# A trunk of two attention layers: a fixed TensorE order for the first attention, gates spread over its groups, and four shared PSUM banks

## Chip, cores and metric

The kernel runs on one core of a Trainium2 chip. The metric is the device time in microseconds (us), of which the median over runs is given. The engines are TensorE (PE in the profile, its weight loads PEld), VectorE (DVE), ScalarE (ACT), GpSimd (POOL) and SyncE (SP, which issues the transfers). All times of the trace come from one profiled execution.

## What is computed

A residual stream x of 512 positions by 1024 channels goes through two layers in f32. Cut to what matters:

```
# layer 1: multi-head latent attention (16 heads of 64 + 32 rotary channels)
proj = rmsnorm(x) @ w_in                      # c_q 384, c_kv 256, k_rope 32, gate 1024
q = rmsnorm(c_q) @ w_q_up                     # 16 heads x 96
k_nope, v = split(rmsnorm(c_kv) @ w_kv_up)    # 16 heads x 64 each
k = concat(k_nope, k_rope of all heads)
q, k = rmsnorm per head, then rope on the last 32
o = causal_softmax_attention(q, k, v)         # 4 blocks of 128 queries
x = x + (o * silu(gate)) @ w_out
x = x + sigmoid(x @ ple_w_gate) * (p @ ple_w_proj)      # embedding part
k_sh, v_sh = split(rmsnorm(x) @ w_kv_shared)
# layer 2: stick-breaking attention on k_sh, v_sh
q, gate = split(rmsnorm(x) @ w_in)
x = x + (stick_breaking(q, k_sh, v_sh) * silu(gate)) @ w_out
x = x + sigmoid(x @ ple_w_gate) * (p @ ple_w_proj)
```

## The kernel before

**Products.** Activations lie transposed: channels on the 128 partitions, 512 positions along the free axis. Every f32 product is three TensorE products of rounded halves, hi x hi, hi x lo and lo x hi (`mm3`, L136). The halves of a weight tile come from `split_w` (L142): ScalarE rounds (`wh`, L147), then VectorE or GpSimd, whichever `lo_engine` names, subtracts (`wl`, L148). A gemm chunk (`gemm_gen`, L179) loads one weight tile `ws`, splits it, multiplies it with eight activation tiles into one PSUM bank and evacuates it. `yield` cuts it into steps that a caller can place between other work.

**Stages.** `mla_in` (L313, to about 41 us) computes c_q and c_kv and ends with the sums of squares (`stats`, L374) and the row R of 1/rms (`row_of`, L202, used by the gate evacuations). `k_rope` (L404) computes the shared rotary part of k. `mla_group(g)` (L453) computes q, k and v of four heads: four query chunks of nine products and four kv chunks of six. Between and behind them lies a chain on other engines: sums of squares on VectorE, a power on GpSimd (`rq`, L478, and `rk`, L505), rope on GpSimd (L308 to L311), and multiplications of k on VectorE (L511, L513). Only then can the heads be transposed. Group 0 and four of the eight gate chunks (`GATES[0]` = 4) are computed ahead of the attention.

**First attention** (`layer`, L787, about 77 to 270 us). It runs over 64 pairs of head and query block in turns. In a turn stand, each for a later pair than the one behind it: for the first block of a head the transposes of its q and k (`mla_prep`, `head_t`, L523, tag t), the scores and the softmax (`mla_front`, L581, tag s), the transposes of the normalised weights `e` (`pt_evac`, L538, tag t, evacuated by L553 and L554), and at the last block the value products of the head (`av`, L556, tag o, evacuated by L574 and L575). Between them, steps of other work are drawn from a generator: the next group, gates, and halves of the output projection. This places instructions only in the program; a scheduler decides the order on each engine from priorities. Attention work has one (`MLA_PRIO`, 50 ahead), and fill products have one behind (`MLA_FILL`).

**PSUM.** There are eight banks: two each of g and s, three of t, and one of o. The bank o holds one value product at a time, in both attentions, and `row_of` and the statistics too.

**The rest.** Output projection and embedding (`out_ple`, `pp_gemm`, 270 to 345 us), then the second attention (`sb_layer`, L682, 388 to 617 us), then the output again. In the second attention TensorE's order is not left to the scheduler: with `lin` set, `pe` (L120) ties each product or transpose to the one before. Its turns name quotas of fill steps at six places.

Of the kernel before, what the change touches and what calls it, by code (L numbers as in the profile page):

```python
# [56 lines left out]
SPREAD_PLE = "gstt"  # L57
# [26 lines left out]
class Trunk:  # L84
    def __init__(self, ctx, tc, A):
# [9 lines left out]
    BUFS = {"A": 8, "B": 10, "qk": 8, "hat": 6, "gate": 8, "v": 2, "f": 6, "e": 12, "ws": 3, "wh": 2, "wl": 2, "R": 1,  # L95
            "sm": 16, "smg": 3, "g": 2, "s": 2, "t": 3, "o": 1}
# [82 lines left out]
    def gemm_gen(self, w_dram, m, acts, evac, gain=None, k0=0, k1=NK, parts=1, fine=False):  # L179
# [10 lines left out]
        for i in range(parts):  # L190
            cs = slice(i * w, (i + 1) * w)
            ps = self.gps([P, w])
            for k in range(nk):
                xh, xl = acts[k0 + k]
                with self.pri(self.mp):
                    self.mm3(ps, wh[:, k], wl[:, k], xh[:, cs], xl[:, cs], k == 0, k == nk - 1)
                if (fine or k == NK // 2 - 1) and k < nk - 1:
                    yield
# [3 lines left out]
    def row_of(self, col):  # L202
        nc = self.nc
        ps = self.ps([P, S], "o")
# [108 lines left out]
    def mla_in(self):  # L313
# [60 lines left out]
        sps = self.ps([P, 3, NT], "o")  # L374
# [78 lines left out]
    def mla_group(self, g, res):  # L453
# [7 lines left out]
        for t in range(NT):  # L461
            ts = slice(t * P, (t + 1) * P)
            ps = self.gps([P, GH * QK])
            for k in range(3):
                ch, cl = self.cq[k]
                with self.pri(self.mp):
                    self.mm3(ps, ch[:, ts], cl[:, ts], wqh[:, k], wql[:, k], k == 0, k == 2)
# [20 lines left out]
        for t in range(NT):  # L488
            ts = slice(t * P, (t + 1) * P)
            ps = self.gps([P, 2, GH, HD])  # L490
            for k in range(2):
                ch, cl = self.ckv[k]
                with self.pri(self.mp):
                    self.mm3(ps, ch[:, ts], cl[:, ts], wkh[:, k], wkl[:, k], k == 0, k == 1)
# [28 lines left out]
    def head_t(self, src, hh, scale):  # L523
        nc = self.nc
        ps = self.ps([QK, S], "t")
        for t in range(NT):
            nc.tensor.transpose(ps[:, t * P:(t + 1) * P], src[hh // 2][:, t, hh % 2], self.ident)  # L527
# [28 lines left out]
    def av(self, h, V):  # L556
# [3 lines left out]
        ps = self.ps([P, S], "o")  # L560
# [43 lines left out]
    def sb_group(self, g, res):  # L604
# [13 lines left out]
        for m in (2 * g, 2 * g + 1):  # L618
            yield from self.gemm_gen(A["w_k"][m], m, self.x2, k_evac, gkv, fine=True)
            yield  # L620
        for m in (2 * g, 2 * g + 1):
            yield from self.gemm_gen(A["w_sq"][m], m, self.x2, q_evac, gsb, fine=True)
# [103 lines left out]
    def pp_gemm(self, i, halves=(0, 1), early="B", fine=False):  # L726
# [7 lines left out]
        for half in halves:  # L734
# [3 lines left out]
            for mc in range(4):  # L738
                ps = self.gps([P, S])
                for k in range(2):  # L740
                    xh, xl = pacts[k]
                    self.mm3(ps, wh[:, mc, k], wl[:, mc, k], xh, xl, k == 0, k == 1)
                    if fine and k == 0:
                        yield
# [3 lines left out]
                if fine or mc % 2:  # L748
                    yield

    def out_half(self, m, w_out, resid, tag):
# [7 lines left out]
        self.gemm_chunk(w_out[m], m, self.og, evac, k0=0, k1=NK // 2)  # L759
# [27 lines left out]
    def layer(self, windows, prep, front, pair, prep_lead, lead, av_lag, off):  # L787
        hp = self.tc.high_priority
# [3 lines left out]
        done = [0] * NG  # L792
        for i in range(-prep_lead, NS + lead + av_lag):
            ip = i + prep_lead
            if ip < NS:
                g = ip // GS
                if ip % NT == 0:
                    with hp(offset=off[0]):
                        heads[ip // NT] = prep(ip // NT, *self.groups[g])
                n, gen = windows[g]  # L800
                while done[g] * GS < n * (ip % GS + 1):
                    next(gen, None)
                    done[g] += 1
                if ip % GS == GS - 1:
                    for _ in gen:
                        pass
            if 0 <= i < NS:
                with hp(offset=off[1]):
                    es[i] = front(i // NT, i % NT, *heads[i // NT])
            b = i - lead  # L810
            if 0 <= b < NS:
                h, j = divmod(b, NT)
                if j > 0:
                    with hp(offset=off[2]):
                        self.pt_evac(h, j - 1, es.pop(b), es.pop(b - 1) if j == 1 else None)
            c = b - av_lag
            if 0 <= c < NS and c % NT == NT - 1:
                h = c // NT
                with hp(offset=off[3]):
                    self.av(h, heads[h][-1])  # L820
                if h % 2:
                    pair(h // 2)

    def chain(self, *parts):
        for p in parts:
            if callable(p):
                p()
                yield
            else:
# [191 lines left out]
```

## Time and profile before

| | |
|---|---|
| median of 3 runs | 712.2 us (709.18 to 715.35) |
| the profiled execution | 711.81 us |
| its span | 710.0 us, 10006 instructions |
| mean granted TensorE clock | 0.975 |
| TensorE busy | 674.5 us, 95% |
| first attention, 77.1 to 270.0 | 192.9 us |
| second attention, 385 to 600 | 215.0 us of it |

A busy TensorE is not one at its best: products overlap, so a row's duration is longer than the distance to the next. The clock is the share of full speed that the throttle granted. In a row, `g<-A,wh` reads output tile from input tiles, and `[1.77 <-DVE gate L575]` says that the engine had been idle for 1.77 us until VectorE's instruction of line 575 ended.

### The profile page before, as it was taken

What the parts mean: (1) busy time and instruction counts of PE and PEld (TensorE: products, weight loads), DVE (VectorE), ACT (ScalarE), POOL (GpSimd) and SP (SyncE); (2) the same over time, 40 slices, a digit from 0 to 9 for tenths busy, and PEclk for the clock granted to TensorE, in tenths of its full rate; (3) what the DMA queues carried; (4) which work ended last, traced back from release to release, by engine and by line L of the source; (5) the groups of instructions that cost most, each with busy time, mean ns of one, the idle gap of its engine ahead of it and who ended that gap; (6) DMA issues with size and microseconds to landing.
All of it is one profiled execution on the core that took longest, in us unless ns stands there. A gap on an engine that the chain in (4) does not pass through costs nothing.

```text
span 710.0 us, 10006 instructions
## 1 busy us (share of the span) xinstructions
PE 674.5 (95%) x3558; PEld 563.7 (79%) x3558; DVE 485.6 (68%) x931; ACT 402.0 (57%) x807; POOL 358.0 (50%) x293
## 2 busy tenths in 40 slices
PE   9799999999979999999899999999999998899997
PEld 6588888879868888888688788778788676688886
DVE  6748499979976865646655777876886797744432
ACT  7256596958986855354434567556565566422321
POOL 5729566755795441036642755663673776100131
PEclk9999999989998999999899999999999999899999
DMA  6242212000023222545232222122111223143231
GB/s 232 57 142 92 89 35 63 30 31 16 16 72 109 88 60 75 163 131 164 95 93 86 87 60 61 59 80 70 60 59 44 77 90 118 60 132 105 88 120 60
DMA packets 21617, 59.81 MB, mean 84 GB/s; under 512 B 2880, under 2 KB 3392, under 8 KB 21568
## 3 DMA queue, kind: packets, MB, share of 16 engines
q1 hardware_dynamic: 21568, 59.18, 26.5%
q8 instruction: 28, 0.46, 0.3%
q14 instruction: 21, 0.17, 0.1%
HBM read 54.97 MB, written 4.19 MB: 83 GB/s over the span
## 4 chain that ended last, share of the span: by engine, by line
PE 61%; DVE 17%; issue 11%; ACT 6%; POOL 2%; DMA 2%; SPq 0%; ACTq 0%; DVEq 0%; POOLq 0%
PE g L131 32%; PE s L131 11%; PE t L131 9%; PE o L131 4%; DVE e L678 3%; PE t L134 3%; DVE wl L148 3%; ACT wh L147 1%; DVE ptl L554 1%; PE t L527 1%; DVE e L590 1%; ACT e L594 1%; DMA e<-in_xT 1%; DVE A L168 1%; DVE A L165 1%
## 5 line engine op out<-in xcount | busy, mean ns | idle before, releaser
L131 PE MATMUL g<-A,wh 128*128 128x512 f32 x576 | 189.7, 411 | 11.0 <-DVE gate L437 4.9
L147 ACT CAST wh<-ws 128x1024 fp32r<-128x1024 f32 (+2 forms) x92 | 90.5, 983 | 112.7 <-issue 53.3
L131 PEld LDWEIGHTS g<-A,wh 128*128 128x128 f32 x576 | 105.4, 194 | 35.6 <-issue 8.3
L148 DVE TENSOR_TENSOR wl<-ws,wh 128x1024 fp32r<-128x1024 f32 (+2 forms) x72 | 99.8, 1387 | 48.6 <-ACT wh L147 46.9
L131 PE MATMUL g<-A,wl 128*128 128x512 f32 x288 | 115.0, 404 | 2.3 <-DVE wl L148 1.9
L186 POOL TENSOR_TENSOR ws<-ws,gc 128x1024 f32<-128x1024 f32 x24 | 51.7, 2156 | 60.1 <-DMA ws<-in_w_sq 29.2
L679 POOL TENSOR_TENSOR e<-e,e 128x384 f32<-128x384 f32 (+1 forms) x48 | 61.7, 1303 | 22.0 <-DVE e L678 14.3
L553 ACT CAST pth<-t 128x384 fp32r<-128x384 f32 (+1 forms) x96 | 49.3, 518 | 40.6 <-PE t L134 40.0
L131 PEld LDWEIGHTS g<-A,wl 128*128 128x128 f32 x288 | 55.6, 194 | 15.3 <-DVE wl L148 2.4
L554 DVE TENSOR_TENSOR ptl<-t,pth 128x384 fp32r<-128x384 f32 (+1 forms) x96 | 56.4, 592 | 14.1 <-ACT pth L553 13.9
L134 PE MATMUL t<-ident,e 128*128 128x128 f32 x320 | 55.5, 274 | 1.3 <-DVE sm L596 1.1
L678 DVE TENSOR_TENSOR_SCAN e<-e,maskb 128x384 f32<-128x384 f32 (+1 forms) x32 | 49.7, 1593 | 8.3 <-ACT e L667 8.2
L148 POOL TENSOR_TENSOR wl<-ws,wh 128x1024 fp32r<-128x1024 f32 (+2 forms) x20 | 41.8, 2088 | 25.8 <-ACT wh L147 25.7
L131 PE MATMUL t<-A,wh 128*128 128x512 f32 x160 | 50.3, 395 | 0.0
L131 PE MATMUL o<-pth,v 128*128 128x256 f32 (+2 forms) x128 | 43.5, 350 | 5.0 <-DVE gate L575 4.9
L134 PEld LDWEIGHTS t<-ident,e 128*128 128x128 f32 x320 | 40.6, 141 | 9.0 <-issue 1.5
L594 ACT ACTIVATE e<-e,sm,smg 128x128 f32<-128x128 f32 (+1 forms) x64 | 42.1, 660 | 8.5 <-DVE sm L593 8.2
L131 PE MATMUL g<-wh,B 128*128 128x384 f32 (+1 forms) x136 | 44.1, 379 | 2.6 <-DVE v L521 2.6
L131 PE MATMUL s<-qk,qk 96*128 96x256 f32 (+2 forms) x192 | 43.2, 340 | 0.8 <-ACT qk L531 0.8
L598 POOL TENSOR_SCALAR e<-e,sm 128x384 f32<-128x384 f32 (+3 forms) x48 | 29.8, 627 | 25.7 <-DVE sm L596 24.2
L131 PE MATMUL g<-wh,A 128*128 128x256 f32 x208 | 42.8, 289 | 0.0
L781 POOL TENSOR_TENSOR f<-f,hat 128x512 f32<-128x512 f32 x4 | 7.3, 1828 | 70.0 <-ACT f L779 70.0
(295 smaller groups left out, 1617.0 us busy)
## 6 DMA issues: line engine op xcount, KB each, us to landing
ws<-in_w_pg SPq DMA_DIRECT2D x16, 512.0 KB, 3.5
ws<-in_w_g SPq DMA_DIRECT2D x8, 512.0 KB, 3.2
ws<-in_w_o SPq DMA_DIRECT2D x16, 256.0 KB, 2.6
ws<-in_w_k SPq DMA_DIRECT2D x8, 512.0 KB, 3.5
ws<-in_w_sq SPq DMA_DIRECT2D x8, 512.0 KB, 3.6
ws<-in_w_v SPq DMA_DIRECT2D x8, 512.0 KB, 3.5
ws<-in_w_sg SPq DMA_DIRECT2D x8, 512.0 KB, 3.6
ws<-in_w_o SPq DMA_DIRECT2D x8, 512.0 KB, 3.6
```

The costliest lines, as they stand in the source:

```text
L131: return self.pe(self.nc.tensor.matmul(*a, **kw))
L134: return self.pe(self.nc.tensor.transpose(*a))
L147: nc.scalar.copy(out=wh, in_=src)
L148: lo_engine.tensor_tensor(out=wl, in0=src, in1=f32(wh), op=ALU.subtract)
L186: nc.gpsimd.tensor_tensor(out=ws, in0=ws, in1=gain.unsqueeze(2).to_broadcast((P, nk, P)), op=ALU.mult)
L553: nc.scalar.copy(out=views[0], in_=ps)
L554: nc.vector.tensor_tensor(out=views[1], in0=ps, in1=f32(views[0]), op=ALU.subtract)
L594: nc.scalar.activation(e[:, 0:n], e[:, 0:n], AF.Exp, bias=st[:, 1:2], scale=sm[:, 2, i:i + 1], accum_out=st[:, 2:3])
L598: nc.gpsimd.tensor_scalar(out=e[:, 0:n], in0=e[:, 0:n], scalar1=st[:, 3:4], scalar2=1.0, op0=ALU.mult, op1=ALU.mult)
L678: v.tensor_tensor_scan(out=x, data0=x, data1=mask[:, ::-1], initial=0.0, op0=ALU.mult, op1=ALU.max)
L679: nc.gpsimd.tensor_tensor(out=b[:, 0:n], in0=b[:, 0:n], in1=om[:, 1:n + 1], op=ALU.mult)
L781: e.tensor_tensor(out=g, in0=g, in1=self.ppt[m][:, cs], op=ALU.mult)
```

## The change

`mla_layer` takes the place of `layer`. With `lin` set, the order in which its turns name TensorE's instructions is the order on the engine. A turn has four places for fill steps, and its quota is shared between them. The numbers of scheduler priority for attention and fill go; weight loads, splits and evacuations of fill work keep one (`MLA_PREP`, 60 ahead). No gates are computed ahead of the attention: gates 0 and 1 open the first window, and the others are spread over three windows, ahead of and behind the group that each window computes. The sigmoids of the gates stand at the ends of windows. `gemm_gen`, `mla_group` and `pp_gemm` yield after nearly each input tile. The bank o goes; t has four, and value products, statistics and `row_of` use t. All gate splits in the attention are on GpSimd, since `lo_engine` is set to it before the first. `e` has 8 buffers instead of 12, `wh` and `wl` have 3 instead of 2. Line numbers of the changed kernel are about 8 lower.

```diff
-MLA_PRIO = (50, 50, 50, 50)
-MLA_FILL = (0, 100)
+MLA_PREP = 60
-GATES = (4, 1, 1, 2, 0)
-HALVES = (0, 0, 2, 6)
-EMBEDS = (0, 8, 9)
-SPREAD_PLE = "gstt"
+SPREAD_PLE = "gsttt"
...
-    BUFS = {... "e": 12, "ws": 3, "wh": 2, "wl": 2, ... "g": 2, "s": 2, "t": 3, "o": 1}
+    BUFS = {... "e": 8, "ws": 3, "wh": 3, "wl": 3, ... "g": 2, "s": 2, "t": 4}
...
     def row_of(self, col):
-        ps = self.ps([P, S], "o")
+        ps = self.ps([P, S], "t")
...
     def av(self, h, V):
-        ps = self.ps([P, S], "o")
+        ps = self.ps([P, S], "t")
...
+    def mla_layer(self, windows, pair):
+        prep_lead, lead, av_lag = MLA_LEAD
...
+            w = min(ip // GS, len(windows) - 1)
+            n, gen = windows[w]
+            turns = GS if w < NG else lead + av_lag
+            step = ip - w * GS
+            quota = n * (step + 1) // turns - n * step // turns
+            marks = [quota * x // 4 for x in range(5)]
+            def fill(a):
+                for _ in range(marks[a + 1] - marks[a]):
+                    next(gen, None)
+            if ip < NS and ip % NT == 0:
+                heads[ip // NT] = self.mla_prep(ip // NT, *self.groups[ip // GS])
+            fill(0)
+            if 0 <= i < NS:
+                es[i] = self.mla_front(i // NT, i % NT, *heads[i // NT])
+            fill(1)
...
+                    self.pt_evac(h, j - 1, es.pop(b), es.pop(b - 1) if j == 1 else None)
+            fill(2)
...
+                self.av(h, heads[h][-1])
+                if h % 2:
+                    pair(h // 2)
+            fill(3)
...
     def run(self):
...
-        for m in range(GATES[0]):
-            for _ in gate1(m, True):
-                pass
...
+        windows = [(45, self.chain(gates(0, 1), grp(1), gates(2, silu=(0, 1, 2)))),
+                   (45, self.chain(gates(3, 4), grp(2), gates(5, silu=(3, 4, 5)))),
+                   (46, self.chain(gates(6, 7, silu=(6, 7)), grp(3), half(0), half(1))),
+                   (30, self.chain(*[half(m) for m in range(2, NK)])),
+                   (17, self.pp_gemm(0))]
-        self.wp, self.mp = MLA_FILL
+        self.lin, self.wp = True, MLA_PREP
         self.lo_engine = nc.gpsimd
-        self.layer(windows, self.mla_prep, self.mla_front, self.gated, *MLA_LEAD, MLA_PRIO)
+        self.mla_layer(windows, self.gated)
+        self.lin, self.wp = False, 0
```

TensorE at the start of the attention. Before, the last kv chunk (s108) is followed by the transposes of R (o71) and the first products of gate 0 (t113):

```order
L131 MATMUL s108_657<-wh97_608,B67_387 128x512
L131 MATMUL s108_657<-wl98_609,B67_387 128x512
L131 MATMUL s108_657<-wh97_608,B68_388 128x512
L206 MATMUL o71_419<-ident_81,sxkv_415 128x128 x4
L131 MATMUL t113_686<-A10_126,wh111_682 128x512 x2
L131 MATMUL t113_686<-A10_126,wl112_683 128x512
```

Later there, one product of gate 3 (t131) stands ahead of the transposes of head 0, q from hat83 and k from hat99:

```order
L131 MATMUL s125_758<-A52_331,wl124_755 128x512
L131 MATMUL t131_794<-A10_126,wh129_790 128x512
L527 MATMUL t134_824<-ident_81,hat83_530 96x128 x4
L527 MATMUL t137_833<-ident_81,hat99_612 96x128 x4
L131 MATMUL t131_794<-A10_126,wh129_790 128x512
L131 MATMUL t131_794<-A10_126,wl130_791 128x512
```

In the changed kernel the same place reads (g119 is gate 0):

```order
L123 MATMUL s108_657<-wl98_609,B67_387 128x512
L123 MATMUL s108_657<-wh97_608,B68_388 128x512
L126 MATMUL t110_680<-ident_81,hat83_530 96x128 x4
L126 MATMUL t113_689<-ident_81,hat99_612 96x128 x4
L123 MATMUL g119_704<-A10_126,wh117_700 128x512 x2
L123 MATMUL g119_704<-A10_126,wl118_701 128x512
```

The transposes of head 0 moved from behind 73 gate products to directly behind the last kv chunk. Ahead of it on TensorE, before, the products of `k_rope` (t75, L414) follow the end of `mla_in` (t6) and stand before the first query chunk:

```order
L131 MATMUL t6_119<-A52_331,wh50_327 128x512 x2
L131 MATMUL t6_119<-A52_331,wl51_328 128x512
L377 MATMUL o70_394<-ones_86,f7_120 128x1 x2
L414 MATMUL t75_434<-A10_126,wh74_431 64x512 x2
L414 MATMUL t75_434<-A17_158,wh74_431 64x512 x2
```

In the changed kernel they follow the last sums of squares (L368) and the transposes of R (t71, L197), behind the first kv chunk (s102); the last query chunk comes after them:

```order
L123 MATMUL s102_615<-wl98_609,B67_387 128x512
L123 MATMUL s102_615<-wh97_608,B68_388 128x512
L368 MATMUL t70_394<-ones_86,f57_365 128x1 x4
L368 MATMUL t70_394<-ones_86,f66_385 128x1 x4
L197 MATMUL t71_419<-ident_81,sxkv_415 128x128 x4
L405 MATMUL t75_434<-A10_126,wh74_431 64x512 x2
```

`k_rope` moved behind three query chunks and one kv chunk, and the transposes of R ahead of it.

GpSimd at the same place, before: power of q (smg85, L478), rope of hat83 and hat84, power of k (L505), and the first gating by a sigmoid (gate114):

```order
L478 TENSOR_TENSOR smg85_532<-smg85_532,mhalf_88 128x16
L310 TENSOR_TENSOR hat83_530<-hat83_530,ct0_506 128x8x32
L310 TENSOR_TENSOR hat84_531<-hat84_531,ct0_506 128x8x32
L311 TENSOR_TENSOR hat83_530<-hat83_530,f94_596 128x8x32
L505 TENSOR_TENSOR smg85_532<-smg85_532,mhalf_88 128x16
L311 TENSOR_TENSOR hat84_531<-hat84_531,f95_601 128x8x32
L445 TENSOR_TENSOR gate114_711<-gate114_711,f115_713 128x512
```

In the changed kernel (powers at L470 and L498, splits at L140):

```order
L470 TENSOR_TENSOR smg85_532<-smg85_532,mhalf_88 128x16
L301 TENSOR_TENSOR hat83_530<-hat83_530,ct0_506 128x8x32
L140 TENSOR_TENSOR wl123_734<-ws121_731,wh122_733 128x1024
L301 TENSOR_TENSOR hat84_531<-hat84_531,ct0_506 128x8x32
L302 TENSOR_TENSOR hat83_530<-hat83_530,f94_596 128x8x32
L498 TENSOR_TENSOR smg85_532<-smg85_532,mhalf_88 128x16
L140 TENSOR_TENSOR wl143_818<-ws141_815,wh142_817 128x1152
```

Two weight splits have come in: that of gate 1 (wl123) between the two powers, and that of group 1 (wl143) behind the second.

VectorE in the second attention, before: two scans (e1152, e1153), then the two evacuations of a value product (from o1160 and o1163) with one of transposed weights between them:

```order
L678 SCALAR_TENSOR_TENSOR e1152_5900<-e1152_5900,maskb_66 128x384
L678 SCALAR_TENSOR_TENSOR e1153_5901<-e1153_5901,maskb_66 128x384
L575 TENSOR_TENSOR gate1161_5934<-o1160_5925,gate1161_5934 64x512
L554 TENSOR_TENSOR ptl0_108<-t1162_5946,pth0_106 128x384
L575 TENSOR_TENSOR gate1161_5934<-o1163_5955,gate1161_5934 64x512
```

In the changed kernel:

```order
L671 SCALAR_TENSOR_TENSOR e1152_5900<-e1152_5900,maskb_66 128x384
L671 SCALAR_TENSOR_TENSOR e1153_5901<-e1153_5901,maskb_66 128x384
L568 TENSOR_TENSOR gate1161_5934<-t1160_5925,gate1161_5934 64x512
L157 TENSOR_TENSOR B1232_6328<-ws1230_6325,B1231_6327 128x512
L547 TENSOR_TENSOR ptl0_108<-t1162_5946,pth0_106 128x384
L157 TENSOR_TENSOR B1234_6332<-ws1230_6325,B1233_6331 128x512
L568 TENSOR_TENSOR gate1161_5934<-t1163_5955,gate1161_5934 64x512
```

The evacuations stand where they did, with the source now in t; two splits of activations have come between them.

## Rows read from the trace of the kernel before

**Rows 1.** Page part 1: busy us, share, instructions of each engine.

```profile
PE 674.5 (95%) x3558; PEld 563.7 (79%) x3558; DVE 485.6 (68%) x931; ACT 402.0 (57%) x807; POOL 358.0 (50%) x293
```

**Rows 2.** Windows by stage.

```profile
core 0: us, PE busy (x) PEld busy (x) DVE busy (x) ACT busy (x) POOL busy (x), PEclk, DMA share, GB/s
59.30:76.10 16.80, 16.80 (x78) 13.96 (x77) 12.56 (x21) 8.13 (x16) 12.07 (x8) 1.00 0.37 128
77.10:270.00 192.90, 182.29 (x1030) 158.92 (x1029) 155.55 (x453) 146.83 (x353) 122.08 (x115) 0.96 0.17 53
142.50:149.30 6.80, 5.92 (x14) 4.67 (x15) 4.87 (x17) 2.75 (x11) 1.41 (x3) 0.50 0.00 1
170.00:201.00 31.00, 30.04 (x179) 26.28 (x178) 26.05 (x93) 28.19 (x73) 24.88 (x28) 1.00 0.05 16
212.60:217.60 5.00, 5.00 (x13) 4.03 (x14) 3.05 (x5) 1.64 (x3) 1.80 (x2) 0.50 0.79 264
385.00:600.00 215.00, 206.59 (x1219) 169.19 (x1218) 164.82 (x252) 129.85 (x250) 129.19 (x83) 0.99 0.23 69
```

**Rows 3.** Waits of TensorE, 77 to 270 (us in total, times, longest).

```profile
PE g L131 <- DVE gate L437: 4.9, 1, 4.9
```

**Rows 4.** Waits of TensorE, 385 to 620.

```profile
PE o L131 <- DVE gate L575: 4.9, 4, 2.2
```

**Rows 5.** Timeline of TensorE, 41 to 78 (start us, us, what).

```profile
41.44 3.86 PE L414 MATMUL t<-A,wh 128*64 128x512 f32 x16
...
59.08 0.39 PE L131 MATMUL s<-wh,B 128*128 128x512 f32 x1
...
59.66 0.71 PE L131 MATMUL t<-A,wh 128*128 128x512 f32 x2
...
76.32 1.03 PE L527 MATMUL t<-ident,hat 128*96 128x128 f32 x8
77.11 0.48 PE L131 MATMUL t<-A,wh 128*128 128x512 f32 x1
```

**Rows 6.** Timeline of GpSimd, 47 to 68.

```profile
47.50 1.39 POOL L372 TENSOR_TENSOR f<-f,f 128x512 f32<-128x512 f32 x1 [0.95 <-ACT f L371]
...
56.37 0.46 POOL L308 TENSOR_TENSOR f<-hat,st 128x128 f32<-128x128 f32 x1
...
59.05 2.89 POOL L478 TENSOR_TENSOR smg<-smg,mhalf 128x16 f32<-128x16 f32 x1
...
64.14 3.82 POOL L505 TENSOR_TENSOR smg<-smg,mhalf 128x16 f32<-128x16 f32 x1
```

**Rows 7.** Timeline of VectorE, 68 to 72.

```profile
68.74 2.36 DVE L511 TENSOR_TENSOR hat<-hat,smg 128x512 f32<-128x512 f32 x2
71.03 0.74 DVE L513 TENSOR_TENSOR hat<-krot,smg 128x256 f32<-128x256 f32 x2
```

**Rows 8.** Timeline of ScalarE, 52 to 57.

```profile
52.02 0.27 ACT L421 COPY kr<-t 128x128 f32<-128x128 f32 x1 [4.15 <-PE t L419]
...
54.76 0.49 ACT L469 ACTIVATE f<-t 128x384 f32<-128x384 f32 x1 [0.82 <-PE t L131]
...
55.94 0.58 ACT L471 COPY hat<-g 128x192 f32<-128x192 f32 x2
```

**Rows 9.** Lines by form, 60 to 270 (xcount, busy us, mean ns, idle).

```profile
L148 POOL TENSOR_TENSOR wl<-ws,wh 128x1024 fp32r<-128x1024 f32 x9 | 22.1, 2455 | 13.5 <-ACT wh L147 13.5
```

**Rows 10.** One line: multiplication of k (ns min, median, max; starts).

```profile
L511 DVE TENSOR_TENSOR hat<-hat,smg x6: 675/678/1760, 68.7 to 159.4; 128x512 f32<-128x512 f32 x6
```

**Rows 11.** Timeline of VectorE, 560 to 563.

```profile
560.21 1.97 DVE L678 TENSOR_TENSOR_SCAN e<-e,maskb 128x384 f32<-128x384 f32 x1
562.11 0.66 DVE L575 TENSOR_TENSOR gate<-o,gate 64x512 f32<-64x512 f32 x1
562.69 0.54 DVE L554 TENSOR_TENSOR ptl<-t,pth 128x384 fp32r<-128x384 f32 x1
```

**Rows 12.** Timeline of TensorE at 562.

```profile
562.82 0.50 PE L131 MATMUL o<-pth,v 128*128 128x512 f32 x1 [1.77 <-DVE gate L575]
```

More of the change, by code (lines that the diff above doesn't have):

```diff
@@ L194, in gemm_gen @@
                 xh, xl = acts[k0 + k]
-                with self.pri(self.mp):
-                    self.mm3(ps, wh[:, k], wl[:, k], xh[:, cs], xl[:, cs], k == 0, k == nk - 1)
-                if (fine or k == NK // 2 - 1) and k < nk - 1:
+                self.mm3(ps, wh[:, k], wl[:, k], xh[:, cs], xl[:, cs], k == 0, k == nk - 1)
+                if k < nk - 1:
                     yield
@@ L465, in mla_group @@
                 ch, cl = self.cq[k]
-                with self.pri(self.mp):
-                    self.mm3(ps, ch[:, ts], cl[:, ts], wqh[:, k], wql[:, k], k == 0, k == 2)
+                self.mm3(ps, ch[:, ts], cl[:, ts], wqh[:, k], wql[:, k], k == 0, k == 2)
+                if k < 2:
+                    yield
             sq = self.t([P, GH, QK], F32, "f")
@@ L492, in mla_group @@
                 ch, cl = self.ckv[k]
-                with self.pri(self.mp):
-                    self.mm3(ps, ch[:, ts], cl[:, ts], wkh[:, k], wkl[:, k], k == 0, k == 1)
+                self.mm3(ps, ch[:, ts], cl[:, ts], wkh[:, k], wkl[:, k], k == 0, k == 1)
+                if k == 0:
+                    yield
             sq = self.t([P, GH, HD], F32, "f")
@@ L724, in sb_layer, with pp_gemm @@
                     pass
-    def pp_gemm(self, i, halves=(0, 1), early="B", fine=False):
+    def pp_gemm(self, i, halves=(0, 1), early="B"):
         nc, A = self.nc, self.A
@@ L742, in pp_gemm @@
                     self.mm3(ps, wh[:, mc, k], wl[:, mc, k], xh, xl, k == 0, k == 1)
-                    if fine and k == 0:
+                    if k == 0:
                         yield
@@ L818, in layer @@
                 h = c // NT
-                with hp(offset=off[3]):
-                    self.av(h, heads[h][-1])
+                self.av(h, heads[h][-1])
                 if h % 2:
                     pair(h // 2)
+            fill(3)
+            if w < NG and step == GS - 1 or i == NS + lead + av_lag - 1:
+                for _ in gen:
+                    pass
     def chain(self, *parts):
         for p in parts:
[L826 to L829, printed above, removed]
-                yield from p
-                yield
+            yield from p
+            yield
     def run(self):
@@ L847, in half, with gates @@
         def half(m):
-            self.out_half(m, A["w_o"][0], self.xres, "gate" if m < NK // 2 else "hat")
-        def gate1(m, act):
-            yield from self.gemm_gen(A["w_g"][m], m, self.xacts, self.gate_raw(self.R1, "gate"))
-            if act:
-                self.silu(m)
-        def silus():
-            for m in range(GATES[0], NK):
+            return self.out_half(m, A["w_o"][0], self.xres, "gate" if m < NK // 2 else "hat")
+        def gates(*ms, silu=()):
+            for m in ms:
+                yield from self.gemm_gen(A["w_g"][m], m, self.xacts, self.gate_raw(self.R1, "gate"))
+                yield
+            for m in silu:
                 self.silu(m)
@@ L933, in gate2 @@
         def gate2(m):
[L934 removed]
+            yield from self.gemm_gen(A["w_sg"][m], m, self.x2, self.gate_raw(self.R2, "f"), gsb)
             self.silu(m)
```

71 lines of the change are left out of this document (12 added, 59 removed).

## The prediction, made before the result was known

> **What bounds the kernel now.** I read the page first: TensorE is busy for 95% of the span, the next engine for 68% [rows 1]. So time is won only where TensorE stands still or runs slowly, and lost wherever it is made to wait. Next came windows by stage [rows 2]. In the first attention (77.1 to 270.0) TensorE is busy for 182.29 of 192.90 us, so 10.6 us are idle. Two short stretches there have a granted clock of 0.50, the lower of its two levels: 142.5 to 149.3, with 5.92 us busy, and the 5.00 us after 212.6. That restart follows the longest wait of the stage, 4.9 us [rows 3]. At full clock the work of both would have taken half the time, so the clock costs (5.92 + 5.00)/2 = 5.4 us. This stage therefore holds 10.6 + 5.4 = 16 us that a better order could save. The second attention (385 to 600), whose order is already fixed, has 215.00 − 206.59 = 8.4 us idle at clock 0.99.
>
> Then I asked what TensorE waits for. In the first attention the largest is one wait of 4.9 us for a gate evacuation [rows 3]; in the second it is four waits of 4.9 us in all for VectorE to release the bank o [rows 4]. Last I read the timeline at the start of the attention, because the order of the changed kernel has something else there. TensorE is through with the kv chunks of group 0 at about 59.3 (the last starts at 59.08) and starts gate products at 59.66. Only at 76.32 come the transposes of head 0, and the next product is at 77.11 [rows 5]. The stretch 59.3 to 76.1 is busy without a gap at clock 1.00 [rows 2]. From 59.66 to 76.3 these are 73 products of gates 0 to 3, so 0.227 us each, 16.6 us.
>
> **Start: the cover goes away.** Behind those products runs a chain that TensorE does not show: rope of q and two power operations on GpSimd (56.37 to 67.96) [rows 6], then on VectorE two multiplications of k and two of the rotated part from 68.74 [rows 7]; head 0 needs the first of the last two, which ends at about 71.4. In the changed order the transposes of head 0 stand directly behind the last kv product, and gate 0 behind them. TensorE's order is fixed from there, so everything behind the two transposes waits: all gate products, then all scores. When are they done? The row R and k_rope now stand behind three chunks of q. The square sums end near 48.9 (47.50 + 1.39) [rows 6]; statistics, two powers and four transposes bring R to about 51 (my estimate), and k_rope takes 3.86 us on TensorE [rows 5]. The copy of kr, which started at 52.02 [rows 8], then comes near 56.5, and the copies of q stand behind it on ScalarE. They ended 4.5 us after kr's start (55.94 + 0.58 − 52.02), of which 0.82 was a wait [rows 8]; so q is done at about 60.5, and the kv products end at about 61.6 instead of 59.3. From the first rope operation to the second power GpSimd took 64.14 − 56.37 = 7.8 us [rows 6]. One weight split of a gate now stands inside this chain on GpSimd: 2.455 us [rows 9]. The power takes 3.8 [rows 6], the VectorE tail 71.4 − 67.96 = 3.4 [rows 7]. Sum: 60.5 + 7.8 + 2.45 + 3.8 + 3.4 = 77.95, and 78.4 with the transposes. Against 77.11 that is 1.3 us later, and the 16.6 us of gates are still to be done: **+17.9 us**. TensorE idles from 61.6 to 78, longer than the 4.9 us after which the clock was 0.50 for 5.00 us [rows 2, 3]; the same again costs **+2.5**. Bounds: the chain may be as short as before (rival 1), or each estimate may be late by 3 us.
>
> A second split, of 128x1152, stands directly behind the second power on GpSimd. In the trace, the same VectorE multiplication took 675 ns or up to 1760 [rows 10], the long one among the two at 68.74 where GpSimd had work. I put nothing for it beyond the 3.4 us above, which hold one such long case. The Trainium skill, "SBUF — State Buffer", section "SBUF: two separate sides", says that VectorE and GpSimd share a port pair as an exclusive lock, which a VectorE operation with two SBUF inputs and a GpSimd operation that reads SBUF take for a whole instruction. By it the multiplications would wait out the entire split: 2.455 x 1152/1024 = 2.76 us after the power, then 0.68 + 0.68 and half of 0.74, 4.5 instead of 3.4, and the sum would be 1.1 higher. The trace agrees that the operation stretches; no row of before shows a full block.
>
> **The attention itself.** The counts of instructions hardly change: the same products, transposes and evacuations, in finer turns. The gates are spread over three windows, ahead of each group and behind it, and cover the chain that ends a group. Before's losses go: **−16**. What stays I take from the second attention, which is ordered the same way: without the waits for o, 8.4 − 4.9 = 3.5 us in 215, 1.6%, which on 206 us of products is 3.4. To that come three ends of a group. There one gate (24 products, 5.45 us) and about 4 us of attention stand between the last kv chunk and the first transposes of the next heads, against a chain of 9 to 11 us; I take 1 each. At the end, the last value product, its gating and its split lie open for 2.6 us before the output projection. Each of these is an estimate; together 3.4 + 3 + 2.6 = **+9**. Bounds: 2 us (nothing but the tail) and 20 (as before). The extra loads of ScalarE's function table, at the sigmoids that end a window, lie on an engine that is busy for 57% [rows 1]; the loads of weights go through the same SyncE queue, somewhat earlier, with a DMA share of 0.17 in this stage [rows 2]; three buffers for the weight halves instead of two and eight e instead of twelve I put at nothing, because no wait for these buffers has a row; if wrong, that is part of rival 2.
>
> **Bank o.** At 562.82 TensorE had waited 1.77 us for the evacuation of the value product before, which started only at 562.11: VectorE was in a scan from 560.21 for 1.97 us [rows 11, 12]. The order of VectorE stays, so the evacuation will not come earlier; with four banks TensorE need not wait for that one. But the transposes share these four, and their evacuations stand behind the same scan (at 562.69) [rows 11]. So of 4.9 us I let 3.5 go: **−3.5**, between 0 and −4.9. The Trainium skill, "Perfetto Trace Analysis", section "Matmuls", says that independent groups should rotate through banks so that evacuation overlaps the next group. By it all 4.9 would go and the sum would be 1.4 lower. The trace agrees that one bank waits; no row shows four shared ones.
>
> **Sum**, against the profiled execution of 711.81 us (span 710.0), which lies 0.4 below the median of 712.2 and is taken as equal: 711.8 + 17.9 + 2.5 − 16 + 9 − 3.5 = 721.7, forecast 721.5. About 1% is what a measurement here can tell from no change: 705.1 and 719.3.
>
> **Rivals.** (1) *The cover is hardly needed.* From the end of the kv products to the end of the chain were 71.4 − 59.3 = 12.1 us in the trace; if that holds, the transposes end at 61.6 + 12.1 + 0.5 = 74.2, 2.9 before 77.11, and the start costs 16.6 − 2.9 = 13.7. With a clock loss of 2, only 2 us of waits left in the attention and the full 4.9 from o: 711.8 + 13.7 + 2 − 16 + 2 − 4.9 = 708.6. It is not slower by over 1%, and decides if the first k transposes run before about 74; before 70, with k_rope early, it is below 705. For it: GpSimd has gaps before 56.37. Against: the split inside the chain, and ScalarE's order. (2) *GpSimd becomes the bound inside the windows.* All splits of gates are now on GpSimd; a multiplication of e queued behind one waits up to 2.455 us [rows 9], and with a fixed order TensorE cannot go round it. GpSimd was busy for 24.88 of 31.00 us from 170 to 201, 80% [rows 2]. If about ten splits each hold TensorE for half their time, 12 us come on top: 733. Against: splits come with priority, and the e multiplications run a turn or more ahead. It decides if waits of TensorE for e exceed 5 us. (3) *The bank waits only move*: transposes wait where value products did, and the second attention gains nothing: 721.5 + 3.5 = 725.
>
> **How the numbers follow.** Forecast 0.40, its own range 716 to 727, of which 0.10 lies below 719.3. Rival 1: 0.35, of which 0.15 is below 705.1 and 0.20 within 1%. Rival 2: 0.13. Rival 3: 0.12. So faster 0.15, within 1% 0.10 + 0.20 = 0.30, slower 0.30 + 0.13 + 0.12 = 0.55. The range of 705 to 733 leaves out the 0.15 of rival 1 below it and about 0.05 of rival 2.
>
> **What would show it.** Right: an idle TensorE of 13 to 18 us between the last kv product near 61 and the transposes near 78, followed by a stretch at 0.50; TensorE's idle in the first attention behind it under 10 us; no wait of value products for a gate evacuation near the 48 units of the second attention. The start is wrong if the transposes come before 74; the attention is wrong if its longest waits are for e or a split on GpSimd, or if TensorE still falls to 0.50 there; the bank step is wrong if waits for t have the sum that o had. The whole is wrong if the time is under 716 with the gap as described: then before lost more in its attention than I found.

## The result and the profile after

The changed kernel takes 731.8 us (median of 4, 729.70 to 735.75), the kernel before beside it 713.4: a ratio of 1.027, interval 1.021 to 1.034. It is slower, as forecast (721.5), by 18.5 us instead of 9.3. The time lies inside the range of 705 to 733, but above the 716 to 727 of the forecast case itself. Its profiled execution took 732.32 us with a span of 730.5.

Busy times, the page's part 1 of the changed kernel, to set beside [rows 1]:

```profile
PE 676.2 (93%) x3558; PEld 564.5 (77%) x3558; DVE 494.7 (68%) x927; ACT 409.5 (56%) x812; POOL 360.7 (49%) x297
```

The work is the same; TensorE stands idle for 54.3 us of the span (730.5 − 676.2) instead of 35.5 (710.0 − 674.5), 18.8 more. Where, the start of the second attention tells. Its first scores, in the timelines of TensorE of the kernel before and of the changed one:

```profile
385.61 0.38 PE L131 MATMUL s<-B,qk 64*128 64x256 f32 x1
```

```profile
418.72 0.38 PE L123 MATMUL s<-B,qk 64*128 64x256 f32 x1
```

Ahead of it 33.1 us were lost; behind it, from 324.4 (710.0 − 385.6) to 311.8 (730.5 − 418.7), 12.6 were won. Of the loss, 20.4 us lie at the start of the first attention. The timeline of TensorE there, which answers to [rows 5] (the bracket is the idle time ahead of an instruction):

```profile
50.83 1.11 PE L197 MATMUL t<-ident,sxkv 128*128 128x128 f32 x4 [1.58 <-POOL sxkv L382]
51.60 6.26 PE L405 MATMUL t<-A,wh 128*64 128x512 f32 x16
...
72.44 1.09 PE L126 MATMUL t<-ident,hat 128*96 128x128 f32 x4 [7.57 <-POOL hat L302]
80.22 1.06 PE L126 MATMUL t<-ident,hat 128*96 128x128 f32 x4 [6.70 <-DVE hat L506]
80.94 1.20 PE L123 MATMUL g<-A,wh 128*128 128x512 f32 x2
```

The transposes of q waited 7.57 us, those of k 6.70. Gate 0 began at 80.94, when before 73 gate products were done at 77.11: 16.6 + 3.8 = 20.4. From there to the second attention (the first attention, its output and embedding part, and the start of layer 2) the kernel before took 385.6 − 77.1 = 308.5 us. The changed kernel took 337.8, of which 16.6 are the gates; the rest, 321.2, is 12.7 longer. TensorE's idle time in this stretch went from 13.8 to 23.9 us, which is 10.1 of the 12.7. So 20.4 + 12.7 − 12.6 = 20.5, the difference of the spans.

Windows of the changed kernel, by stage as in [rows 2]: the start, its attention, the first products behind the start, and the second attention:

```profile
59.00:80.20 21.20, 6.95 (x31) 5.43 (x32) 16.96 (x28) 10.38 (x33) 18.93 (x17) 0.69 0.22 71
80.20:308.50 228.30, 210.79 (x1146) 181.28 (x1147) 164.58 (x457) 161.10 (x366) 124.19 (x118) 0.96 0.16 52
80.90:84.20 3.30, 3.30 (x10) 2.66 (x9) 0.69 (x1) 0.58 (x1) 0.00 (x0) 0.54 0.00 0
418.70:633.70 215.00, 210.65 (x1246) 173.94 (x1246) 175.14 (x264) 136.27 (x260) 132.34 (x85) 0.99 0.24 74
```

The first attention is idle for 228.30 − 210.79 = 17.5 us, more than before (10.6), at the same clock of 0.96; the second for 4.3 instead of 8.4. Waits of TensorE in the first attention and the start, the list that answers to [rows 3]:

```profile
PE t L126 <- DVE hat L506: 18.6, 3, 6.7
PE t L126 <- POOL hat L302: 7.6, 1, 7.6
PE g L123 <- DVE v L514: 4.6, 5, 1.7
```

The gate evacuation is gone from the list. Three waits for the multiplication of k stand there instead: the one at 80.22, and one at each of two group ends:

```profile
130.06 1.06 PE L126 MATMUL t<-ident,hat 128*96 128x128 f32 x4 [5.92 <-DVE hat L506]
```

```profile
190.06 1.06 PE L126 MATMUL t<-ident,hat 128*96 128x128 f32 x4 [5.96 <-DVE hat L506]
```

In the second attention the waits for o of [rows 4] have no successor; the whole list is:

```profile
PE g L123 <- DVE f L428: 3.3, 1, 3.3
PE s L123 <- DVE v L514: 1.1, 1, 1.1
```

What a chain to the transposes looks like is best read at the first group end. GpSimd, VectorE and ScalarE of the changed kernel from 116 to 131:

```profile
116.95 2.40 POOL L140 TENSOR_TENSOR wl<-ws,wh 128x1024 fp32r<-128x1024 f32 x1
119.30 2.97 POOL L498 TENSOR_TENSOR smg<-smg,mhalf 128x16 f32<-128x16 f32 x1
...
126.75 2.89 POOL L140 TENSOR_TENSOR wl<-ws,wh 128x1152 fp32r<-128x1152 f32 x1
```

```profile
123.14 0.16 DVE L589 RECIPROCAL sm<-sm 128x1 f32<-128x1 f32 x1 [1.56 <-ACT e L587]
...
125.18 0.16 DVE L589 RECIPROCAL sm<-sm 128x1 f32<-128x1 f32 x1 [1.03 <-ACT e L587]
125.26 0.15 DVE L499 TENSOR_TENSOR smg<-smg,sxkv 128x16 f32<-128x16 f32 x1
...
125.44 1.73 DVE L504 TENSOR_TENSOR hat<-hat,smg 128x512 f32<-128x512 f32 x2
127.09 3.16 DVE L506 TENSOR_TENSOR hat<-krot,smg 128x256 f32<-128x256 f32 x2
```

```profile
118.03 1.28 ACT L435 ACT_TABLE_LOAD   x1
...
121.00 1.28 ACT L587 ACT_TABLE_LOAD   x1
122.30 0.71 ACT L587 ACTIVATE e<-e,sm,smg 128x384 f32<-128x384 f32 x1
...
124.24 0.81 ACT L587 ACTIVATE e<-e,sm,smg 128x512 f32<-128x512 f32 x1 [1.14 <-DVE sm L586]
```

The power (L498) stands behind a weight split of 2.40 us. It ends at 122.27, but the VectorE instruction that reads it (L499) starts only at 125.26, since ahead of it stand two reciprocals that wait for exponentials on ScalarE. The first exponential (122.30) stands behind two table loads of 1.28; the second (124.24) waits for VectorE. Then another split starts at 126.75, and the two instructions of L506, 0.75 us together at 79.67, take 3.16 and end 0.6 us behind it.

### The profile page after: what moved, and what is told of

It reads as the page before. It is cut to its first block, busy times and chain, and to the rows that moved or that the text cites. A ratio compares the mean times of both kernels' runs of the same rounds, so it can differ in the third digit from the quotient of the medians.

```text
span 730.5 us, 10010 instructions
## 1 busy us (share of the span) xinstructions
PE 676.2 (93%) x3558; PEld 564.5 (77%) x3558; DVE 494.7 (68%) x927; ACT 409.5 (56%) x812; POOL 360.7 (49%) x297
## 4 chain that ended last, share of the span: by engine, by line
PE 73%; DVE 6%; ACT 4%; issue 2%; POOL 2%; DMA 1%; ACTq 0%; POOLq 0%; DVEq 0%
PE g L123 38%; PE t L123 17%; PE s L123 12%; PE t L126 6%; DVE wl L140 1%; DVE hat L506 1%; ACT wh L139 1%; DVE A L157 1%; POOL f L879 1%; ACT e L587 1%; ACT L587 1%; DMA ws<-in_w_v 0%; DVE hat L504 0%; DVE smg L499 0%; POOL smg L470 0%
## 5 line engine op out<-in xcount | busy, mean ns | idle before, releaser
L123 PE MATMUL g<-A,wh 128*128 128x512 f32 x624 | 205.0, 411 | 7.3 <-ACT A L156 4.7
L123 PEld LDWEIGHTS g<-A,wh 128*128 128x128 f32 x624 | 111.1, 193 | 30.9 <-ACT A L156 5.4
L123 PE MATMUL g<-A,wl 128*128 128x512 f32 x312 | 123.1, 398 | 0.5 <-POOL wl L339 0.5
L140 DVE TENSOR_TENSOR wl<-ws,wh 128x1024 fp32r<-128x1024 f32 (+2 forms) x68 | 93.8, 1382 | 40.0 <-ACT wh L139 39.4
L123 PEld LDWEIGHTS g<-A,wl 128*128 128x128 f32 x312 | 59.3, 191 | 14.7 <-POOL wl L339 1.1
L140 POOL TENSOR_TENSOR wl<-ws,wh 128x1024 fp32r<-128x1024 f32 (+2 forms) x24 | 49.9, 2079 | 37.9 <-ACT wh L139 37.8
L126 PE MATMUL t<-ident,e 128*128 128x128 f32 x320 | 50.8, 274 | 0.0
L123 PE MATMUL s<-qk,qk 96*128 96x256 f32 (+1 forms) x192 | 43.9, 338 | 0.4 <-DVE sm L583 0.4
L126 PE MATMUL t<-ident,hat 128*96 128x128 f32 x128 | 19.1, 292 | 26.5 <-DVE hat L506 18.6
L123 PE MATMUL t<-pth,v 128*128 128x256 f32 (+2 forms) x128 | 40.3, 326 | 0.0
```

The costliest lines, as they stand in the source:

```text
L123: return self.pe(self.nc.tensor.matmul(*a, **kw))
L126: return self.pe(self.nc.tensor.transpose(*a))
L140: lo_engine.tensor_tensor(out=wl, in0=src, in1=f32(wh), op=ALU.subtract)
```

## Experiments

Each changes one kernel in one place, unless said. The table has, of each profiled execution, the start of the transposes of k of head 0 (the middle of the row where q and k share one), the first scores of the second attention, the span, and what lies between these two; then the median of its runs and the ratio, with its interval, to the kernel before run beside it (median 713.4 for the changed kernel, 710.1 for e1 to e4, 711 for e5 to e8, 710.4 for e9 to e12). There are 2 to 10 runs of each and one trace. In six traces whose code behind the first scores is the same (changed, e1, e5 to e8), the column "from there" agrees within 0.5 us.

| run | k | 2nd att. | span | from there | median | ratio |
|---|---|---|---|---|---|---|
| before | 76.8 | 385.6 | 710.0 | 324.4 | 713.4 | |
| changed | 80.2 | 418.7 | 730.5 | 311.8 | 731.8 | 1.027 (1.021–1.034) |
| e1 two gates ahead | 81.1 | 407.7 | 719.3 | 311.6 | 724.8 | 1.022 (1.015–1.029) |
| e2 bank o back | 69.0 | 409.0 | 724.7 | 315.7 | 727.4 | 1.025 (1.022–1.029) |
| e3 before, t has four | 82.7 | 387.6 | 703.8 | 316.2 | 709.5 | 0.999 (0.996–1.002) |
| e4 before, weight buffers | 74.2 | 379.6 | 695.3 | 315.7 | 697.7 | 0.984 (0.980–0.987) |
| e5 row behind k_rope | 73.0 | 410.6 | 722.5 | 311.9 | 725.2 | 1.019 (1.013–1.026) |
| e6 sigmoids moved | 80.3 | 419.1 | 730.8 | 311.7 | 731.8 | 1.029 (1.024–1.034) |
| e7 splits on VectorE | 78.5 | 401.7 | 713.8 | 312.1 | 715.7 | 1.007 (1.000–1.014) |
| e8 three edits | 79.2 | 405.1 | 716.9 | 311.8 | 720.8 | 1.013 (1.000–1.026) |
| e9 before, all buffers | 80.6 | 394.7 | 707.6 | 312.9 | 702.4 | 0.986 (0.982–0.989) |
| e10 order repaired | 73.4 | 387.7 | 700.8 | 313.1 | 702.9 | 0.989 (0.986–0.993) |
| e11 before, eight e | 77.7 | 387.0 | 709.5 | 322.5 | 710.9 | 1.001 (0.998–1.004) |
| e12 scheduler's order | 81.4 | 396.9 | 709.4 | 312.5 | 714.3 | 1.006 (1.003–1.009) |

**e1: gates 0 and 1 ahead of the attention.**

```diff
+        for _ in gates(0, 1):
+            pass
-        windows = [(45, self.chain(gates(0, 1), grp(1), gates(2, silu=(0, 1, 2)))),
+        windows = [(29, self.chain(grp(1), gates(2, silu=(0, 1, 2)))),
```

> Changed kernel, but gates 0 and 1 are computed ahead of the first attention again, behind group 0, instead of at the head of its first window. My theory (the cover of the start is what was lost): 48 products of 0.227 us, 10.9 us, run while the chain to the first transposes of k goes on, so TensorE's waits before them fall from 14 us to about 3 to 5 and the time falls by 9 to 13 us, to 719 to 723. Rival (the chain is pushed back by whatever stands ahead of it): the transposes of k come 8 us or more later than at 80, and the gain is under 4 us, 728 or more.

The second attention begins 11.0 us earlier, and the median fell by 7, less than forecast. At the start 10.0 are won: the 10.9 of 48 products, less 0.9 by which the transposes of k come later. So the cover was what was lost. But the waits there fell only from 14.3 to 8.1 us, not to 3 to 5, and here is why: behind the power stood two splits (74.72 on GpSimd, 4.62 us together), beside which the VectorE instructions L499 and L500, 0.15 and 0.17 us at the first group end, took 2.31 and 2.37. The last 1.0 is a balance: the first window is now another, its wait of 5.92 at the group end is gone, and waits of 3.07 for e and 1.47 for transposed weights are new.

**e2: the bank o back, in the changed kernel; e3: the bank o given to t, in the kernel before.**

```diff
-            "sm": 16, "smg": 3, "g": 2, "s": 2, "t": 4}
+            "sm": 16, "smg": 3, "g": 2, "s": 2, "t": 3, "o": 1}
...
-        ps = self.ps([P, S], "t")
+        ps = self.ps([P, S], "o")
```

> Changed kernel, but value products, statistics and row_of get their own bank o again and t has three. My theory (one bank for the value products cost the second attention waits, and behind them half clock): the stretch from the first scores to the last value product of the second attention gets 8 to 12 us longer, with waits for an evacuation of value products of about 5 us in the list; the first attention changes by less than 5; about 742. Rival (the third buffer of the weight halves made the second attention faster): that stretch changes by less than 3 us, about 732.

> Kernel before, with the bank o given to t (t has four) and nothing else. My theory: the second attention gets 8 to 12 us shorter, waits of value products for an evacuation vanish, and the first attention, left to the scheduler, stays within 4 us: 700 to 706. Rival (buffers of weight halves, not the bank): the second attention changes by less than 3 us, 709 or more.

Without the shared banks the changed kernel takes 3.9 us more from the first scores on, not 8 to 12, so the bank is not all of its gain. And the start came 11.2 us earlier (69.0 against 80.2), which neither theory had: sharing the bank had moved `k_rope`, which starts at 37.64 here and at 51.60 in the changed kernel, and R. In the kernel before, the bank alone does give 8.2 us behind the first scores, and the waits for o are gone; the list of the second attention then reads:

```profile
PE g L131 <- DVE f L437: 3.3, 1, 3.3
PE g L131 <- DVE wl L148: 2.3, 2, 1.2
PE s L131 <- DVE v L521: 1.1, 1, 1.1
```

But its transposes of k come 5.9 us later (82.7), and over ten runs nothing is won (0.999), where I had expected 700 to 706. The profiled execution, with a span of 703.8, was the fastest of the ten, while that of the kernel before (711.81 us) is slower than its 710.1 here, so the two spans show more than the runs do. Where the others lose what the second attention wins is not in it; the later start is the one loss that it shows.

**e4: three buffers of each weight half and eight e, in the kernel before; e11: eight e alone.**

```diff
-"e": 12, "ws": 3, "wh": 2, "wl": 2
+"e": 8, "ws": 3, "wh": 3, "wl": 3
```

> Kernel before, with three buffers of each weight half instead of two and eight e instead of twelve. My theory: no change beyond 3 us in either attention, about 713. Rival (weight buffers): the second attention gets 7 us or more shorter, about 705, and the waits for wl there (2.3 us) vanish.

> Kernel before with eight e instead of twelve and nothing else (weight halves keep two buffers). My theory: the third weight buffer made the run with both faster, so here nothing is won: 708 to 715, the second attention with its waits for o of 4.9 and for wl of 2.3 us. Rival (fewer e change the scheduler's order for the better): 703 or less.

My theory fell. The buffers alone make the kernel before 1.6% faster (two runs), the fastest of all; e11, inside its range, shows that fewer e alone win nothing, so it is the weight halves. In the second attention of e4 the waits for wl are gone, and those for o have halved:

```profile
PE g L131 <- DVE f L437: 3.3, 1, 3.3
PE o L131 <- DVE gate L575: 2.6, 4, 0.9
```

So the gain of the second attention has two sources that overlap: 8.2 by the bank alone, 8.7 by the buffers alone, 12.6 by both. The buffers win another 6.0 us ahead of it (379.6 against 385.6).

**e5: R behind k_rope, in the changed kernel.**

```diff
-        self.R1 = self.row_of(self.sx)
...
         self.k_rope()
+        self.R1 = self.row_of(self.sx)
```

> Changed kernel, with row_of called behind k_rope instead of ahead of it; nothing else. My theory: value products, statistics, R and k_rope take banks from one ring of t in the order of the program, so k_rope had to wait for the statistics and R, which before had the bank o. Then k_rope comes directly behind the input products again, the transposes of k of head 0 come at 69 to 72 instead of 80.2, and the span falls by 8 to 11 us, to about 720 to 722. Rival (the chain of powers on GpSimd sets the start, whatever k_rope does): the transposes come at 77 or later and the span falls by under 4.

The transposes of k come 7.2 us earlier, a little later than forecast, and the span is 8.0 shorter. In its order `k_rope` stands directly behind the input products again (at 37.72), as before the change. So it had been held up by taking its bank of t behind R, which waits for the statistics.

**e6: sigmoids moved; e7: splits on VectorE, each in the changed kernel.**

```diff
-        windows = [(45, self.chain(gates(0, 1), grp(1), gates(2, silu=(0, 1, 2)))),
-                   (45, self.chain(gates(3, 4), grp(2), gates(5, silu=(3, 4, 5)))),
-                   (46, self.chain(gates(6, 7, silu=(6, 7)), grp(3), half(0), half(1))),
+        windows = [(45, self.chain(gates(0, 1, silu=(0, 1)), grp(1), gates(2))),
+                   (45, self.chain(gates(3, 4, silu=(2, 3, 4)), grp(2), gates(5))),
+                   (46, self.chain(gates(6, 7, silu=(5, 6, 7)), grp(3), half(0), half(1))),
```

```diff
-        self.lo_engine = nc.gpsimd
         self.mla_layer(windows, self.gated)
```

> Changed kernel, with the sigmoids of gates 0 to 5 taken from the ends of the first two windows and put ahead of the group products of a window, so that no function table is loaded beside the chain that ends a group. My theory: of the waits of 5.9 us for the multiplications of k at 130 and 190, about 3 us each are VectorE's queue behind a reciprocal that waits for ScalarE's exponential and its table loads; each wait falls to 2 to 4, and the span by 5 to 8 with the clock behind them: 722 to 727. Rival (splits on GpSimd alone set these waits): they stay above 5 us and the span within 3.

> Changed kernel, with the weight splits of the first attention on VectorE instead of GpSimd. My theory: at the group ends one split stands ahead of the power on GpSimd (2.4 us) and one holds VectorE's multiplication for its length (3.16 instead of 0.74 us); without them the waits at 130 and 190 fall from 5.9 to 1 to 3.5 us each, the transposes of k of head 0 come 3 to 5 us earlier, and the span falls by 8 to 14: 717 to 723. Rival (VectorE, then busy with some 17 us more, is late for e and for evacuations): new waits for VectorE of 8 us or more spread over the windows, no gain.

With the sigmoids moved the two waits fell to 4.55 and 4.27 us, and nothing was won, against 5 to 8 forecast: 2.9 us of waits for a copy by ScalarE (L463) came in the list. With the splits on VectorE, the span falls by 16.7, more than forecast; 1.7 of it is at the transposes of k at the start, 15.3 between these and the second attention. The wait at the first group end has shrunk to 0.25 us, and the second is this:

```profile
175.83 0.61 PE L126 MATMUL t<-ident,hat 128*96 128x128 f32 x4 [0.26 <-DVE hat L506]
```

VectorE has more work and no list shows new waits for it. So the splits on GpSimd made the group ends. How much of that was the split ahead of the power and how much the one that held the multiplications of k, no run separates.

**e8: e5 together with the later windows of e6, and gates 0 and 1 with their sigmoids ahead of the attention.**

```diff
         self.k_rope()
+        self.R1 = self.row_of(self.sx)
...
+        for _ in gates(0, 1, silu=(0, 1)):
+            pass
-        windows = [(45, self.chain(gates(0, 1), grp(1), gates(2, silu=(0, 1, 2)))),
+        windows = [(29, self.chain(grp(1), gates(2))),
```

> Changed kernel with three edits together: row_of behind k_rope, gates 0 and 1 with their sigmoids ahead of the attention, and the other sigmoids moved as in the run that moves them alone. My theory (the three losses are separate): 10 us for the row, 7 to 9 for the gates (the chain is shorter now, so the cover is worth less), 5 to 8 for the sigmoids: 704 to 711. Rival (they overlap, since a shorter chain at the start only uncovers the next wait): 715 or more.

Missed by 10; the rival's 715 or more came. The transposes of k came at 79.2, not at 73.0 as with the row alone (e5). The timelines of GpSimd and VectorE before them show why:

```profile
63.58 2.67 POOL L140 TENSOR_TENSOR wl<-ws,wh 128x1152 fp32r<-128x1152 f32 x1
66.21 1.43 POOL L302 TENSOR_TENSOR hat<-hat,f 128x256 f32<-128x256 f32 x2
67.60 2.35 POOL L140 TENSOR_TENSOR wl<-ws,wh 128x1024 fp32r<-128x1024 f32 x1
69.91 2.90 POOL L497 TENSOR_TENSOR smg<-smg,mhalf 128x16 f32<-128x16 f32 x1
72.78 1.26 POOL L435 TENSOR_TENSOR gate<-gate,f 128x512 f32<-128x512 f32 x1
74.00 2.34 POOL L140 TENSOR_TENSOR wl<-ws,wh 128x1024 fp32r<-128x1024 f32 x1
```

```profile
74.00 2.37 DVE L499 TENSOR_TENSOR smg<-smg,sxkv 128x16 f32<-128x16 f32 x1
76.29 2.42 DVE L503 TENSOR_TENSOR hat<-hat,smg 128x512 f32<-128x512 f32 x2
```

Two splits, of 2.67 and 2.35 us, stood ahead of the power; but two, of 2.34 and 2.61, stand there in e5 too, where the power starts at 67.58. That is 2.3 of the 6.2 us. The other 3.9 lie behind the power: a gating and a third split stand there on GpSimd, and L499, 0.16 us in e5, took 2.37 beside the split. The products ahead of the attention do not only cover the chain: what they bring to GpSimd also lengthens it.

**e9: the kernel before with all buffers and banks of the change and e5's edit; e10: the changed kernel with e1, e5 and e7; e12: the changed kernel with TensorE left to the scheduler in the first attention (its edit also keeps the fixed order on in the last output, behind the second attention).**

```diff
-        self.lin, self.wp = True, MLA_PREP
+        self.wp = MLA_PREP
```

> Kernel before, its order of TensorE left to the scheduler, with three buffers of each weight half, eight e, four banks t instead of t and o, and row_of behind k_rope. My theory (buffers and banks are what the second attention gains by, together 12 us there; the buffers gained 6 us ahead of it; with row_of behind k_rope four banks cost nothing at the start): 692 to 697, faster than both kernels. Rival (the scheduler's first attention loses with four shared banks what the second wins, as with four banks alone): 698 to 704.

> Changed kernel with its fixed order, row_of behind k_rope, the products of gates 0 and 1 ahead of the attention (sigmoids left in the first window), and all splits of the first attention on VectorE. My theory (the fixed order itself costs nothing; the uncovered start and the splits on GpSimd did): 713.8 of span with the splits alone, less 7 to 10 for the gates and 4 to 7 for the row: 695 to 704. Rival (a fixed order waits for whatever is late next): a new wait of 5 us or more at the start or at a group end, 706 or more.

> Changed kernel without the fixed order in the first attention: the same turns, buffers and banks, but the scheduler decides TensorE's order there. My theory (the fixed order made TensorE wait at the start with gate products ready behind the transposes): the scheduler draws gates forward, the waits of 7.6 and 6.7 us at the start and of 5.9 at the group ends shrink to under 3 each, and the time falls by 15 us or more, under 717. Rival (chains on GpSimd and VectorE bound the stage whatever TensorE's order): within 6 us of 731.8.

e10 lies in its range: with a covered start (a wait of 4.8 for k stays there), and without splits on GpSimd, the fixed order is 1.1% faster than the kernel before. e9 is as fast (702.4 against 702.9), so with these buffers and banks the fixed order, as repaired here, is no faster than the scheduler's, and neither reaches the 697.7 of e4. My theory for e9, 692 to 697, missed; its rival's 698 to 704 came. It is slower than e4, which has the bank o: its profiled execution waits 4.3 us for the multiplications of k at 80.6. That execution was the longest of its five, so the row of e9 in the table is worse than its median. e12 is the direct test of the order: with the scheduler alone the median falls by 17.5 us, and the second attention begins 21.8 earlier. The waits at the group ends are gone; one of 6.2 at its start stays, which I expected under 3.

## Why the prediction was right, and where its sizes were off

The forecast of slower held, and most of its sizes did not.

*The start*, +17.9, measured 20.4. The chain ran as written, 2.3 us later (80.22 against 77.95). R came at 51.98, forecast 51. k_rope took 6.26 us instead of 3.86: TensorE had waited 1.58 us shortly before it and ran at a granted clock of 0.50 from 51.6 to 56. GpSimd also did gate 0's split (59.50, 2.41 us) ahead of the rope, which I had left out. Its rope of q began at 63.44 instead of 60.5. The splits about the second power and VectorE behind it read:

```profile
68.67 2.34 POOL L140 TENSOR_TENSOR wl<-ws,wh 128x1024 fp32r<-128x1024 f32 x1
...
72.33 2.91 POOL L498 TENSOR_TENSOR smg<-smg,mhalf 128x16 f32<-128x16 f32 x1
75.21 2.62 POOL L140 TENSOR_TENSOR wl<-ws,wh 128x1152 fp32r<-128x1152 f32 x1
```

```profile
68.67 2.38 DVE L496 TENSOR_TENSOR smg<-smg,statw 128x16 f32<-128x16 f32 x1
...
75.28 2.58 DVE L499 TENSOR_TENSOR smg<-smg,sxkv 128x16 f32<-128x16 f32 x1 [0.25 <-POOL smg L498]
77.78 0.76 DVE L500 TENSOR_TENSOR smg<-smg,sxkv 128x16 f32<-128x16 f32 x1
78.46 1.28 DVE L504 TENSOR_TENSOR hat<-hat,smg 128x512 f32<-128x512 f32 x2
79.67 0.75 DVE L506 TENSOR_TENSOR hat<-krot,smg 128x256 f32<-128x256 f32 x2
```

The tail behind the power was 80.04 − 75.24 = 4.8 us, for which I had put 3.4. Two terms went the other way: from the first rope of q to the power it took 8.9 us with a split in it, forecast 10.25, and the power 2.91, forecast 3.8. So 2.9 and 1.4 too little stood against 1.4 and 0.9 too much; that the sum came within 2.3 is partly luck. That R and k_rope come later I had read from the order; why, I had not asked. e2 and e5 show that it is the price of the shared ring of banks, 7 to 11 us at the transposes of k.

*The clock behind the idle start*, +2.5: the 3.3 us behind it were at 0.54, so 1.5 us; more at the group ends.

*The attention itself*, −16 + 9, failed. With the clock, it came to +12.7 (up to the second attention) where I had −4.5, a miss of 17. Two of the signs that I had set down came: an idle time of 17.5 us in the first attention instead of under 10, and a clock at 0.50 again, for 3 to 5 us behind two group ends. The step that failed is the one on the three ends of a group at 1 us each. Two measured 5.92 and 5.96. I compared a cover of 9.5 us with a chain of 9 to 11, and left out what would stand in that chain's queues: a split ahead of the power, the table loads ahead of the exponential that VectorE waits for, and a second split that held the multiplication of k. I had named the splits, but in rival 2, holding the multiplications of e. That was the right engine and the wrong victim: no wait for e is in the list, though the time, 731.8, is close to rival 2's 733. e7 shows the size, 15.3 us in this stretch. The third end, where k is multiplied on GpSimd, waited 0.4, and the open end before the output projection 2.8, forecast 2.6.

*Bank o*, −3.5, measured −12.6 from the first scores of the second attention to the end. Of this, 7.8 are idle time (16.2 us before, 8.4 after); the rest is shorter busy time, in part from the clock, which before was at 0.50 for 3 us behind the longest wait for o (2.20 us, to 589.83). The waits for o went, as forecast, and rival 3 is out: no wait for t came. But I had put three weight buffers at nothing, "because no wait for these buffers has a row", though the list of the kernel before, from which [rows 4] shows one line, has this one too:

```profile
PE g L131 <- DVE wl L148: 2.3, 2, 1.2
```

That was the second step that failed. e4 shows 8.7 us from the second attention on and 12 in all (697.7 against 710.1). The errors, +2.5 at the start, +17.2 and −9.1, leave 10.6: that the two large ones half cancelled, and the time came out nearer than its parts, is luck.

*The port and the banks.* For a lock of the port shared by VectorE and GpSimd I had named 1.1 us, outside the sum; the tail was 1.4 longer than I had put. L499 took 2.58 us, 0.15 at the first group end, and ended with the split beside it; in e10, without splits on GpSimd, the instruction in its place took 0.17. The Trainium skill, "SBUF — State Buffer", section "SBUF: two separate sides", says that the loser of the shared port waits for the whole instruction; these rows agree, and it should have been in the sum. The Trainium skill, "Perfetto Trace Analysis", section "Matmuls", says that independent groups should rotate through banks; the waits for o went, which agrees. But the sharing that came with it cost more at the start than it gave: e2, with a bank of its own for o, begins the second attention 9.7 us earlier, loses 3.9 from there on, and is 5.8 shorter in all.

## What to carry to other kernels

Before an engine's order is fixed, write down for every transpose or product at a stage border the chain that it waits for on other engines, with all that stands in their queues ahead of each link. Work that the scheduler drew forward to cover that chain has to be placed by hand. When tags of a pool are merged, look at what else was in the old bank: the ring hands banks out in program order, so a late reader of one tile holds up the next. Of a bundle of edits, run each alone: the best part of this one was one more buffer for each weight half, which came with the change in passing.

## What was not expected of the hardware

VectorE instructions with two inputs in SBUF took as long as GpSimd's splits that ran beside them: 2.38 us for one that took 0.41 elsewhere, beside a split of 2.34; 2.58 for one of 0.15, beside 2.62; and 3.16 for two of 0.75 together, beside 2.89. In these three the size of the operation did not matter. Behind the idle stretches of 5.9 to 6.7 us TensorE's granted clock was 0.50, the lower of its two levels, for 3 to 5 us each time.
